# Hybrid GLA / neighbourhood / GQA backbone on one core: four split buffer pairs, low parts in halves, an estimated clock with the shared port, and regrouped GLA output products

## The chip, the cores and the metric

The kernel runs on one core of a Trainium2 chip. The metric is the time on the device, in microseconds, of one execution of the whole program. The profile is of one such execution, taken by the hardware profiler. Engines are named as the profile names them: PE is TensorE (its weight loads are PEld), DVE is VectorE, ACT is ScalarE, POOL is GpSimd, SP is SyncE, which issues most DMAs.

## The reference

Two layers of a diffusion backbone are computed over 256 latent tokens (x) and 256 context tokens (ctx) of width 1024. One layer is:

```
x = x + 0.5 * g1 * swiglu(modulate(rms_norm(x), sh1, sc1))          # FFN of width 2816; the same for ctx
p = modulate(rms_norm(x), sh2, sc2) @ w_in                          # 10784 columns
y = sum over 3 branches of sigmoid(gate_i) * (branch_i(p) @ w_branch[i]),  then @ w_out
x = x + g2 * y
x = x + 0.5 * g3 * swiglu(modulate(rms_norm(x), sh3, sc3))          # second FFN
```

The branches are a gated linear attention in both directions (GLA, 4 heads, chunks of 64 tokens), a neighbourhood attention (16 heads) and a grouped-query attention with rotary positions (GQA, 8 heads). The shifts, scales and gates come from `silu(c) @ w_mod + b_mod`, 9216 columns for each layer ("mods" below). In the second layer the context tokens are needed as keys and values alone. All is float32.

## The kernel before, in words

Tokens stand on the free axis, features on the partitions, so a weight tile of 128 x 128 is loaded into PE and 512 or 256 token columns are streamed. Float32 products of full precision are made from three products of the faster type float32r: each operand is split into a rounded high part and a low part (value minus high part), and `mm3` issues high x high, high x low and low x high into one PSUM bank.

Weights arrive in 504 chunks of 128 x 1024 (the `w_raw` tiles, 512 KB; a few are half as long). For each chunk `splitter` in `Program.run` lets ACT write the high part (`w_hi`, a cast) and POOL the low part (`w_lo`, one subtraction of 1024 columns a partition; in the first four chunks four of 256). `SPLIT_BUFS` = 3 pairs of `w_hi` and `w_lo` buffers go round, so the cast of a chunk waits until PE is done with the chunk three before it. `SPLIT_AHEAD` = 2 says how many chunks the recording may run ahead. Three raw buffers (`RAW_BUFS`) go round in front of that. Where a pair of chunks is needed at once (the first chunks of an FFN, the q and k projections of GLA in `proj_f2`, the last projection of `merge_out`), a chunk is marked "kept", and its buffers come free one chunk later.

The main line of the program is a list of chunks, each with the matmuls that use it (`up` and `dn` in the FFN, `pf` and `pt` in the projections). All else is a "side": generators for the mods (`mod_gen`, whose sums `mod_acc` are made on DVE), the norms (`norm_chain`), the splits of activations, the GLA heads (`gla_head`) and the attention heads (`attn_weights`, `attn_values`, with `head_norm` ahead of them). After every few matmuls `tick` asks every side whether its next instruction may be recorded now. That is decided by an estimated clock (class `Clock`): `took` gives each instruction a duration, `emit` adds it to its engine's time, and `Gated` lets a side's instruction in when its operands are ready by that clock (on PE with a margin of 0.5 us). So the durations in `took` set the order in which all engines' instructions stand. That order is then fixed, and on the chip each engine runs its own list in order and waits by semaphores.

The names that the steps below use: `rs_*` are the tiles of `rsqrt` (some ten small DVE operations, one behind the other), `a_s` the scores of attention in PSUM, `a_mx` their maxima, `a_p` the weights, `a_t` their transposes, `n_tab` the neighbourhood tables that POOL makes, `g_o` the outputs of GLA (`out_mm` in `gla_head`), `ff_h` the FFN's hidden values. Small tiles of 2 KB a partition come from one pool of `SLOTS` = 54.

Of the kernel before, what the change touches and what calls it, by code (L numbers as in the profile page):

```python
# [18 lines left out]
P = 128  # L19
# [17 lines left out]
C_GATE = 7712  # L37

RAW_BUFS = 3
SPLIT_BUFS = 3  # L40
SPLIT_AHEAD = 2
SLOTS = 54
LANES = 2
PE_MARGIN = 0.5
OTHER_SLACK = 0.1
QUEUE = 1.0
MOD_PACE = 42.0


def r32(ap):  # L50
    return ap.bitcast(F32R)


class Clock:
# [59 lines left out]
    def took(self, engine, name, ins, outs):  # L114
        n = max([x.free_size() for x in ins + outs] + [1])
        if engine == "PE":
            return 0.11 if name == "transpose" else self.matmul(ins, outs[0])
        if engine == "ACT":
            return 0.18 + n / 1200 + (0.2 if len(outs) > 1 else 0.0)
        if engine == "POOL":  # L120
            return 0.1 + n * 0.00235
        both = sum(not x.space == bass.MemoryType.PSUM and x.free_size() > 64 for x in ins) > 1
        return 0.15 + n / 960 * (1.8 if both else 1.15)

    def emit(self, engine, name, ins, outs):
        start = max(self.t[engine], self.need(ins, outs))
# [74 lines left out]
class Program:  # L201
# [155 lines left out]
    def run(self):  # L357
        specs = [it[1] for it in self.items if it[0] == "c"]
        raws, parts, ended = {}, {}, {}
        state = {"loaded": 0, "ci": 0}  # L360

        def load(n):
            while state["loaded"] < min(len(specs), n):
                j = state["loaded"]
                src, a, b = specs[j][:3]
                raw = self.rpool.tile([P, a, b], F32, name="w_raw", tag="r", padded_shape=[P, 1024 // b, b])
                old = raws.get(j - RAW_BUFS)
                if old is not None:
                    self.clock.floor[raw.name] = self.clock.read.get(old.name, 0.0)
                self.clock.dma(raw)  # L370
                self.nc.sync.dma_start(raw, src)
                raws[j] = raw
                state["loaded"] += 1

        def splitter():
            for j, (src, a, b, do, halves) in enumerate(specs):
                while j > state["ci"] + SPLIT_AHEAD or (j >= SPLIT_BUFS and j - SPLIT_BUFS not in ended):
                    yield None
                load(j + 1)
                hi = self.wpool.tile([P, a, b], F32, name="w_hi", tag="w", padded_shape=[P, 1024 // b, b])  # L380
                lo = self.wpool.tile([P, a, b], F32, name="w_lo", tag="w", padded_shape=[P, 1024 // b, b])
                self.clock.floor[hi.name] = self.clock.floor[lo.name] = ended.get(j - SPLIT_BUFS, 0.0)
                raw = raws[j]
                yield from self.gact.copy(r32(hi), raw)
                h = a // 4 if halves else a
                for s in range(0, a, h):
                    yield from self.ggp.tensor_tensor(r32(lo[:, s : s + h]), raw[:, s : s + h], hi[:, s : s + h], op=ALU.subtract)
                parts[j] = (r32(hi), r32(lo))
                load(j + 1 + RAW_BUFS)
                if self.force:  # L390
                    yield None

        self.load = load
        split = splitter()

        def advance(g):

            self.first = True
            self._resume(g)
            self.first = False  # L400

        work = self.round

        def round_with_splits():
            n = self.clock.count
            advance(split)
            w = list(self.wakes)
            more = work()
            self.wakes += w
            return more or self.clock.count > n  # L410

        self.round = round_with_splits
        for kind, _, fn in self.items:
            if kind == "f":
                self.flush()
                fn()
                continue
            ci = state["ci"]
            load(ci + 1)
            self.force = True  # L420
            while ci not in parts:
                advance(split)
            self.force = False
            fn(parts.pop(ci))
            if ci + 1 not in self.kept:
                ended[ci] = self.clock.now
            if ci in self.kept:
                ended[ci - 1] = self.clock.now
            state["ci"] = ci + 1
        self.flush()  # L430
        assert not self.sides, list(self.sides)
# [3 lines left out]
def tile_backbone(ctx: ExitStack, tc: tile.TileContext, I: dict, out: bass.AP):  # L435
# [4 lines left out]
    sml = ctx.enter_context(tc.tile_pool(name="sml", bufs=4))  # L440
    slot = ctx.enter_context(tc.tile_pool(name="slot", bufs=SLOTS))
    upool = ctx.enter_context(tc.tile_pool(name="upool", bufs=16))
    rpool = ctx.enter_context(tc.tile_pool(name="rpool", bufs=RAW_BUFS))
    wpool = ctx.enter_context(tc.tile_pool(name="wpool", bufs=2 * SPLIT_BUFS))
    psa = ctx.enter_context(tc.tile_pool(name="psa", bufs=4, space=PS))
# [10 lines left out]
    def S(name):  # L456
        return slot.tile([P, 512], F32, name=name, tag="s")
# [20 lines left out]
    def side_bank(name):  # L478
        t = psd.tile([P, 512], F32, name=name, tag="d")
        if getattr(prog, "floors", None):  # L480
            clock.floor[t.name] = max(prog.floors)
        return t
# [4 lines left out]
    def gmm(o, a, b, start, stop):  # L487
        yield from gpe.matmul(o, a, b, start=start, stop=stop)
# [58 lines left out]
    x = [cst.tile([P, NT], F32, name=f"x{k}") for k in range(KT)]  # L547
# [201 lines left out]
    def mod_side(blocks):  # L749
        st["mod_done"] = set()  # L750
        prog.start(
            "mods", lambda: (mod_gen(blocks[i : i + 2], "mods", MOD_PACE) for i in range(0, len(blocks), 2))
        )
# [486 lines left out]
    def gla_head(l, h, nq):  # L1240
# [4 lines left out]
        v = [st["gv"][t, h // 2][:, (h % 2) * 256 : (h % 2) * 256 + 256] for t in range(TT)]  # L1245
# [131 lines left out]
        at = S("g_at")[:, :nq]  # L1377
        yield from gdve.tensor_tensor(at, att[0], att[1], op=ALU.add)

        state = [dict(), dict()]  # L1380
# [23 lines left out]
        ss = sml.tile([P, TT], F32, name="g_ss", tag="g_ss")  # L1404

        def out_mm(t):
            if t % 2 == 0:
                on[t // 2] = side_bank("g_o")
            po = on[t // 2][:, (t % 2) * 256 : (t % 2) * 256 + 256]
            yield from gmm(po, at[:, t * P : (t + 1) * P], v[t], True, False)  # L1410
            todo = [(half, d) for d in range(2) for half in range(2) if t in state[d]]
            for i, (half, d) in enumerate(todo):
                lhs = qe[d][:, (2 * t + half) * 64 : (2 * t + half + 1) * 64] if half == d else qe2[d][:, t, :]
                yield from gmm(po[64 * half : 64 * half + 64, :], lhs, state[d][t], False, i >= len(todo) - 2)

        def out_ev(tp):
            o = S("g_o32")
# [18 lines left out]
        for tp in reversed(range(ntq // 2)):  # L1436
            yield from prog.banks(1)
            for t in range(2):
                yield from out_mm(2 * tp + t)
            yield from out_ev(tp)  # L1440
            prog.release(1)
            yield from out_ss(tp)
# [588 lines left out]
    for l in range(DEPTH):  # L2031
        last = l == DEPTH - 1
        n = LAT if last else NT
# [51 lines left out]
```

## Time and profile before

| | |
|---|---|
| median of 3 runs | 2831.05 us (2829.24 to 2831.47) |
| the profiled execution's own time | 2831.27 us |
| its span in the profile | 2829.5 us |
| PE busy | 2767.3 us, 98% |
| PE weight loads busy | 2316.6 us, 82% |
| DVE busy | 1669.3 us, 59% |
| ACT busy | 1011.8 us, 36% |
| POOL busy | 1279.1 us, 45% |
| HBM read | 342.83 MB, mean 122 GB/s |
| mean granted TensorE clock | 0.994 of full speed |

The span runs from the first to the last instruction. Busy time is the time in which an engine has an instruction under way, also when that instruction itself is held up. What PE does not spend busy is time in which it waited for something; the profile names what ended each wait. The granted clock is given for each stretch as a share of 2.4 GHz, so a stretch at 1.2 GHz reads 0.50.

### The profile page before, as it was taken

Reading aid. Unit: us, or ns where it says so; the run is one execution under the profiler, and the core shown is the slowest. Engines: PE = TensorE matmul, PEld = TensorE weight load, DVE = VectorE, ACT = ScalarE, POOL = GpSimd, SP = SyncE. Lnnn points to the kernel's source line nnn. Section 1 sums busy time; section 2 is a strip of 40 time slices with the busy share of each in tenths; the row PEclk is TensorE's granted clock in tenths of the full one; section 3 lists DMA queues with packets and bytes.
Section 4 is the critical chain, followed back from the end, with each engine's and each line's share of the span. In section 5 each row is a group of like instructions: output and inputs, shape, how many; then the busy total and the mean of one; then the engine's idle time right before and its main releaser. Section 6 shows DMA issues by size and latency. Waiting matters only on the chain.

```text
span 2829.5 us, 39683 instructions
## 1 busy us (share of the span) xinstructions
PE 2767.3 (98%) x15547; PEld 2316.6 (82%) x15547; DVE 1669.3 (59%) x2956; ACT 1011.8 (36%) x1603; POOL 1279.1 (45%) x591
## 2 busy tenths in 40 slices
PE   8999999999999999999999999999999998999999
PEld 6888888777777788888888888888877777899899
DVE  5655566678766675667555475512554659756422
ACT  3222223433544344322222222222244335564443
POOL 4444442334333443334444434444333455557687
PEclk9999999999999999999999999999999999999999
DMA  7444443224222322433444434433322334435554
GB/s 247 150 145 140 149 138 98 90 82 133 74 74 66 88 75 60 154 129 124 137 142 144 157 116 141 135 97 116 89 78 80 103 102 118 119 105 193 169 183 157
DMA packets 295839, 346.46 MB, mean 122 GB/s; under 512 B 15669, under 2 KB 239062, under 8 KB 295652
## 3 DMA queue, kind: packets, MB, share of 16 engines
q1 hardware_dynamic: 295252, 343.81, 38.8%
q8 instruction: 122, 2.00, 0.3%
q14 instruction: 65, 0.53, 0.1%
q10 hardware_dynamic: 176, 0.07, 0.0%
q0 software_dynamic: 224, 0.05, 0.0%
HBM read 342.83 MB, written 1.05 MB: 122 GB/s over the span
## 4 chain that ended last, share of the span: by engine, by line
PE 87%; DVE 9%; issue 3%; POOL 1%; DMA 1%; ACT 0%; SPq 0%; DVEq 0%; ACTq 0%; POOLq 0%
PE up L169 29%; PE pf L169 17%; PE dn L169 15%; PE pt L169 14%; PE a_s L196 2%; PE a_t L196 2%; PE n_o L196 1%; PE g_o L196 1%; PE q_o L196 1%; POOL w_lo L196 1%; PE g_U L196 1%; DVE a_p L196 1%; DVE n_ss L196 1%; PE a_qk L196 1%; DVE rs_y L196 1%
## 5 line engine op out<-in xcount | busy, mean ns | idle before, releaser
L196 POOL TENSOR_TENSOR w_lo<-w_raw,w_hi 128x1024 fp32r<-128x1024 f32 (+2 forms) x516 | 1219.5, 2369 | 1487.1 <-ACT w_hi L196 1431.5
L196 ACT CAST w_hi<-w_raw 128x1024 fp32r<-128x1024 f32 (+1 forms) x504 | 520.8, 1036 | 945.2 <-issue 286.9
L169 PE MATMUL up<-u_hi,w_hi 128*128 128x512 f32 (+1 forms) x1504 | 530.9, 353 | 2.2 <-DVE u_hi L196 2.1
L169 PE MATMUL up<-u_hi,w_lo 128*128 128x512 f32 (+1 forms) x1504 | 528.7, 352 | 4.0 <-POOL w_lo L196 3.9
L169 PE MATMUL up<-u_lo,w_hi 128*128 128x512 f32 (+1 forms) x1504 | 529.8, 352 | 2.8 <-DVE u_lo L196 2.2
L196 DVE SCALAR_TENSOR_TENSOR mod_acc<-mod_w,scv,mod_acc 128x512 f32<-128x512 f32 x364 | 374.8, 1078 | 53.2 <-DMA mod_w<-w_mod 53.2
L169 PE MATMUL dn<-ff_h,w_hi 128*128 128x512 f32 (+1 forms) x1528 | 397.0, 349 | 0.0
L169 PEld LDWEIGHTS up<-u_hi,w_hi 128*128 128x128 f32 x1504 | 285.2, 190 | 50.4 <-issue 6.7
L169 PEld LDWEIGHTS up<-u_hi,w_lo 128*128 128x128 f32 x1504 | 285.1, 190 | 42.5 <-POOL w_lo L196 5.2
L169 PEld LDWEIGHTS up<-u_lo,w_hi 128*128 128x128 f32 x1504 | 285.2, 190 | 42.2 <-DVE u_lo L196 4.7
L169 PEld LDWEIGHTS dn<-ff_h,w_hi 128*128 128x128 f32 x1528 | 267.5, 189 | 39.8 <-issue 2.5
L169 PE MATMUL dn<-ff_h,w_lo 128*128 128x512 f32 (+1 forms) x764 | 265.9, 348 | 0.0
L169 PE MATMUL pt<-w_hi,u_hi 128*128 128x512 f32 x640 | 261.8, 409 | 0.0
L169 PE MATMUL pf<-u_hi,w_hi 128*128 128x256 f32 (+1 forms) x736 | 250.8, 341 | 5.7 <-DVE u_hi L196 2.2
L169 PE MATMUL pt<-w_hi,u_lo 128*128 128x512 f32 x640 | 251.2, 393 | 0.0
L169 PE MATMUL pt<-w_lo,u_hi 128*128 128x512 f32 x640 | 251.0, 392 | 0.0
L169 PE MATMUL pf<-u_lo,w_hi 128*128 128x256 f32 (+1 forms) x736 | 239.5, 325 | 3.7 <-DVE u_lo L196 2.9
L169 PE MATMUL pf<-u_hi,w_lo 128*128 128x256 f32 (+1 forms) x736 | 238.2, 324 | 4.2 <-POOL w_lo L196 4.2
L169 DVE TENSOR_TENSOR ff_h<-ff_a,up 128x512 f32<-128x512 f32 (+1 forms) x88 | 53.3, 621 | 311.6 <-PE up L169 278.9
L169 PE MATMUL pf<-y,w_hi 128*128 128x512 f32 (+1 forms) x768 | 197.4, 347 | 2.0 <-ACT y L196 1.2
L169 PEld LDWEIGHTS pf<-u_hi,w_hi 128*128 128x128 f32 x736 | 141.8, 193 | 27.3 <-issue 8.3
L169 PEld LDWEIGHTS dn<-ff_h,w_lo 128*128 128x128 f32 x764 | 144.6, 189 | 18.2
(229 smaller groups left out, 3937.9 us busy)
## 6 DMA issues: line engine op xcount, KB each, us to landing
w_raw<-ffn_w_in SPq DMA_DIRECT2D x176, 512.0 KB
w_raw<-w_in SPq DMA_DIRECT2D x168, 512.0 KB
mod_w<-w_mod SPq DMA_DIRECT2D x288, 256.0 KB
w_raw<-ffn_w_out SPq DMA_DIRECT2D x80, 512.0 KB
w_raw<-w_branch SPq DMA_DIRECT2D x48, 512.0 KB
w_raw<-w_out SPq DMA_DIRECT2D x16, 512.0 KB
w_raw<-ffn_w_out SPq DMA_DIRECT2D x16, 256.0 KB
n_rel<-nat_rpb SPq DMA_DIRECT2D x32, 109.5 KB
```

The lines of the kernel that those rows point to most:

```text
L169: return real(*args, **kw)
L196: return real(*args, **kw)
```

## The change

- `SPLIT_BUFS` goes from 3 to 4 and `SPLIT_AHEAD` from 2 to 3: four pairs of split buffers. To make room, `SLOTS` goes from 54 to 52.
- The low part of every chunk is made in two subtractions of half the columns (the first four chunks keep their four).
- The estimated clock gives a DVE instruction 0.15 us plus its elements at 960 per us times 1.1, and another 0.15 us (`PORT_WAIT`) where `shares` finds that all its tensors lie in SBUF and that it reads two of them, or that it is a `tensor_scalar` or a `tensor_copy`. Before, it was 0.15 us plus the elements times 1.8 for two wide SBUF inputs and times 1.15 otherwise.
- In `out_mm` of GLA the product of an odd token tile with 128 output partitions (`at` with `v`) is issued last, behind its products with 64 output partitions, where it was issued first. The start and stop flags move with it.

```diff
-SPLIT_BUFS = 3
-SPLIT_AHEAD = 2
-SLOTS = 54
+SPLIT_BUFS = 4
+SPLIT_AHEAD = 3
+SLOTS = 52
...
+PORT_WAIT = 0.15
...
-        both = sum(not x.space == bass.MemoryType.PSUM and x.free_size() > 64 for x in ins) > 1
-        return 0.15 + n / 960 * (1.8 if both else 1.15)
+        return 0.15 + n / 960 * 1.1 + (PORT_WAIT if self.shares(name, ins, outs) else 0.0)
+
+    @staticmethod
+    def shares(name, ins, outs):
+
+        tensors = [x for x in ins if x.free_size() > 1]
+        if any(x.space == bass.MemoryType.PSUM for x in tensors + outs):
+            return False
+        return len(tensors) > 1 or bool(tensors) and name in ("tensor_scalar", "tensor_copy")
...
-                h = a // 4 if halves else a
+                h = a // 4 if halves else a // 2
...
             po = on[t // 2][:, (t % 2) * 256 : (t % 2) * 256 + 256]
-            yield from gmm(po, at[:, t * P : (t + 1) * P], v[t], True, False)
+            if t % 2 == 0:
+                yield from gmm(po, at[:, t * P : (t + 1) * P], v[t], True, False)
             todo = [(half, d) for d in range(2) for half in range(2) if t in state[d]]
             for i, (half, d) in enumerate(todo):
                 lhs = qe[d][:, (2 * t + half) * 64 : (2 * t + half + 1) * 64] if half == d else qe2[d][:, t, :]
-                yield from gmm(po[64 * half : 64 * half + 64, :], lhs, state[d][t], False, i >= len(todo) - 2)
+                first, last = i < 2 and t % 2 == 1, i >= len(todo) - 2 and t % 2 == 0
+                yield from gmm(po[64 * half : 64 * half + 64, :], lhs, state[d][t], first, last)
+            if t % 2 == 1:
+                yield from gmm(po, at[:, t * P : (t + 1) * P], v[t], False, True)
```

The new durations move instructions all through the program. Three places show how.

PE, one pair of GLA output tiles in the first layer, before:

```order
L196 MATMUL g_o<-g_v,g_at 128x256
L196 MATMUL g_o<-g_S,g_qe 64x256
L196 MATMUL g_o<-g_S,g_half 64x256 x2
L196 MATMUL g_o<-g_S,g_qe 64x256
L196 MATMUL g_o<-g_v,g_at 128x256
L196 MATMUL g_o<-g_S,g_qe 64x256
L196 MATMUL g_o<-g_S,g_half 64x256 x2
L196 MATMUL g_o<-g_S,g_qe 64x256
```

and now:

```order
L204 MATMUL g_o<-g_v,g_at 128x256
L204 MATMUL g_o<-g_S,g_qe 64x256
L204 MATMUL g_o<-g_S,g_half 64x256 x2
L204 MATMUL g_o<-g_S,g_qe 64x256 x2
L204 MATMUL g_o<-g_S,g_half 64x256 x2
L204 MATMUL g_o<-g_S,g_qe 64x256
L204 MATMUL g_o<-g_v,g_at 128x256
```

The eight products with 64 output partitions now stand together, between the two with 128. There are 12 such pairs in the program, and in the changed one nothing stands between their products.

ACT, the second layer, where the GLA gates' projection `fg` has come out and the q and k projections of the next heads begin, before:

```order
654 L169 CAST fg<-fg 32x512 x2
655 L196 CAST w_hi<-w_raw 128x1024
656 L196 ACTIVATE g_abs<-g_z 128x512 x3
657 L196 ACTIVATE g_abs<-g_abs 128x512 x3
658 L196 ACTIVATE g_abs<-g_z 128x512
659 L196 ACTIVATE g_abs<-g_abs 128x512 x4
660 L196 ACTIVATE g_e<-g_G 128x512
661 L196 ACTIVATE g_ei<-g_G 128x512
662 L196 ACTIVATE g_abs<-g_abs 128x512
663 L196 CAST w_hi<-w_raw 128x1024 x2
664 L196 ACTIVATE g_e<-g_G 128x512
```

and now:

```order
660 L177 CAST fg<-fg 32x512 x2
661 L204 CAST w_hi<-w_raw 128x1024
662 L204 ACTIVATE g_abs<-g_z 128x512 x3
663 L204 ACTIVATE g_abs<-g_abs 128x512 x3
664 L204 ACTIVATE g_abs<-g_z 128x512
665 L204 ACTIVATE g_abs<-g_abs 128x512 x4
666 L204 ACTIVATE g_e<-g_G 128x512
667 L204 ACTIVATE g_ei<-g_G 128x512
668 L204 ACTIVATE g_abs<-g_abs 128x512
669 L204 CAST w_hi<-w_raw 128x1024
670 L204 ACTIVATE g_e<-g_G 128x512
```

The rows read alike, but the casts are of later chunks now: counted over ACT's whole list, 332 chunks are cast ahead of the `g_abs` rows where it was 331; at the same place in the first layer it is 80 where it was 79.

DVE, the second layer, behind the rotary `rsqrt` chain of the GQA keys, where two neighbourhood heads have their maxima made (ISA is the fused addition of the table and maximum), before:

```order
1856 L196 TENSOR_TENSOR q_raw<-q_raw,rs_y 128x256 x4
1857 L196 TENSOR_TENSOR q_sw<-q_raw,cossin 128x128 x2
1858 L196 TENSOR_TENSOR q_rot<-q_raw,cossin 128x256
1859 L196 TENSOR_REDUCE a_mx<-a_s 128x1
1860 L196 ISA a_s,a_mx<-a_s,n_tab,a_mx 128x256
1861 L196 ISA a_mx 128x1
1862 L196 TENSOR_SCALAR a_mx<-a_mx 128x1
1863 L196 TENSOR_REDUCE a_mx<-a_s 128x1
1864 L196 TENSOR_TENSOR q_rot<-q_rot,q_sw 128x256
```

and now:

```order
1846 L204 TENSOR_TENSOR q_raw<-q_raw,rs_y 128x256 x4
1847 L204 TENSOR_TENSOR q_sw<-q_raw,cossin 128x128 x2
1848 L204 TENSOR_TENSOR q_rot<-q_raw,cossin 128x256
1849 L177 COPY q_raw<-pt 128x512
1850 L204 TENSOR_REDUCE a_mx<-a_s 128x1 x2
1851 L204 TENSOR_TENSOR q_rot<-q_rot,q_sw 128x256
1852 L204 ISA a_s,a_mx<-a_s,n_tab,a_mx 128x256
1853 L204 ISA a_mx 128x1
1854 L204 ISA a_s,a_mx<-a_s,n_tab,a_mx 128x256
1855 L204 ISA a_mx 128x1
```

The two heads' first scores stand together on PE now, and so do their maxima here. On PE, counted over its list, the two groups of scores of those maxima had 6 `pt` products between them and 30 behind the second until the next scores; now they stand next to each other with 48 behind them.

## Rows read from the trace of the kernel before

**Rows 1.** Page, part 1: busy us (share of the span) xinstructions.

```profile
PE 2767.3 (98%) x15547; PEld 2316.6 (82%) x15547; DVE 1669.3 (59%) x2956; ACT 1011.8 (36%) x1603; POOL 1279.1 (45%) x591
```

**Rows 2.** Windows, PE alone: stretch, length, busy us (x), granted clock, DMA share, GB/s.

```profile
0.00:42.00 42.00, 33.86 (x209) 1.00 0.95 328
406.00:426.00 20.00, 17.50 (x129) 1.00 0.42 119
...
2026.00:2045.00 19.00, 15.20 (x89) 0.91 0.31 87
462.00:490.00 28.00, 24.66 (x191) 0.94 0.30 94
1655.00:1668.00 13.00, 11.42 (x81) 0.87 0.32 103
2074.00:2098.00 24.00, 20.09 (x149) 0.93 0.22 66
2636.00:2642.00 6.00, 4.29 (x35) 1.00 0.23 68
436.00:450.00 14.00, 12.57 (x62) 1.00 0.56 160
...
2300.00:2620.00 320.00, 301.20 (x2211) 0.97 0.45 134
2328.00:2345.00 17.00, 11.45 (x40) 0.80 0.38 113
```

**Rows 3.** Waits of PE, longest first: us in total, times, longest us.

```profile
PE a_s L196 <- ACT a_p L196: 8.1, 3, 3.2
...
PE pf L169 <- POOL w_lo L196: 4.2, 3, 2.0
...
PE pf L169 <- DVE fg L169: 1.8, 2, 0.9
```

**Rows 4.** Timeline, PE, one GLA output pair of layer two: start us, us, instruction.

```profile
2111.49 0.59 PE L196 MATMUL g_o<-g_v,g_at 128*128 128x256 f32 x2
2112.02 0.43 PE L196 MATMUL g_o<-g_S,g_qe 128*64 128x256 f32 x1
...
2112.51 0.38 PE L196 MATMUL g_o<-g_S,g_qe 128*64 128x256 f32 x1
...
2112.72 0.38 PE L196 MATMUL g_o<-g_S,g_qe 128*64 128x256 f32 x1
2113.03 0.70 PE L196 MATMUL g_o<-g_v,g_at 128*128 128x256 f32 x2
2113.66 0.43 PE L196 MATMUL g_o<-g_S,g_qe 128*64 128x256 f32 x1
```

**Rows 5.** Timeline, ACT and PE, 2074 to 2098 us; in brackets idle before, and releaser.

```profile
2088.19 1.99 ACT L196 CAST w_hi<-w_raw 128x1024 fp32r<-128x1024 f32 x2
...
2091.78 0.39 PE L169 MATMUL pf<-u_hi,w_lo 128*128 128x256 f32 x1 [1.99 <-POOL w_lo L196]
```

**Rows 6.** Timeline, DVE and POOL, 2322 to 2329 us.

```profile
2323.65 0.17 DVE L196 TENSOR_TENSOR rs_a<-rs_y,rs_a 128x8 f32<-128x8 f32 x1
2323.85 2.38 DVE L196 SCALAR_TENSOR_TENSOR rs_y<-rs_a,rs_y 128x8 f32<-128x8 f32 x1
2326.26 2.32 DVE L196 TENSOR_TENSOR rs_a<-rs_y,rs_v 128x8 f32<-128x8 f32 x1
...
2323.80 4.75 POOL L196 TENSOR_TENSOR w_lo<-w_raw,w_hi 128x1024 fp32r<-128x1024 f32 x2 [0.62 <-ACT w_hi L196]
```

**Rows 7.** Instructions by tile, DVE: ns min/median/max, first and last start, forms.

```profile
L196 DVE TENSOR_TENSOR ff_h<-ff_h,ff_h x88: 409/1371/2897, 55.9 to 2796.8; 128x512 fp32r<-128x512 f32 x66, 128x256 fp32r<-128x256 f32 x22
```

**Rows 8.** Groups by shape, POOL, whole span: xcount, busy us, mean ns, idle before.

```profile
L196 POOL TENSOR_TENSOR w_lo<-w_raw,w_hi 128x1024 fp32r<-128x1024 f32 x484 | 1185.2, 2453 | 1441.3 <-ACT w_hi L196 1395.6 <-PE g_oT L196 15.6 <-PE q_o L196 8.0
```

**Rows 9.** The same view, 2647 to 2829 us, the last FFN.

```profile
L196 POOL TENSOR_TENSOR w_lo<-w_raw,w_hi 128x1024 fp32r<-128x1024 f32 x59 | 142.4, 2416 | 31.1 <-ACT w_hi L196 26.7 <-DMA w_raw<-ffn_w_out 1.8 <-PE dn L169 1.4
L196 POOL TENSOR_TENSOR w_lo<-w_raw,w_hi 128x512 fp32r<-128x512 f32 x4 | 5.2, 1290 | 0.0
```

## The prediction

> **What bounds the kernel now.** I read the page's busy times first: PE is busy for 2767.3 of 2829.5 us, so the end is set by PE's list, and apart from cheaper PE work only its idle time, 62.2 us, can be won [rows 1]. The reader should then see where that idle time lies. A table of windows with PE alone gives idle (length less busy) and granted clock for each [rows 2].
>
> - Start, 0 to 42 us: 8.1 us, on first loads.
> - Four stretches behind norms (first 406 to 426, last 2026 to 2045): 2.5, 3.2, 1.3 and 3.8, together 10.7 us.
> - Four stretches behind "kept" pairs (462, 1655, 2074, 2636): 3.3, 1.6, 3.9 and 1.7, together 10.5 us.
> - Four stretches of GLA and attention (436 to 450, 490 to 1150, 2098 to 2300, 2300 to 2620): 1.4, 5.1, 2.1 and 18.8, together 27.4 us. Nearly a third of the last lies in one place: 5.55 idle in 2328 to 2345.
>
> A long wait costs twice. In 2328 to 2345 the granted clock is 0.80 on average, that is part of it at 1.2 GHz, after PE had stood still. What the clock took from a stretch is its length times one less the clock: 28 x 0.06 + 13 x 0.13 + 24 x 0.07 = 5.0 us behind kept pairs, 320 x 0.03 = 9.6 us in the last attention stretch, 19 x 0.09 = 1.7 us behind the last norm [rows 2]. The waits view names releasers: ACT `a_p` for the scores, 8.1 us, POOL `w_lo` for projections, 4.2 us, and DVE `fg` twice, 1.8 us [rows 3].
>
> **The change, part by part.**
>
> *GLA products.* In the timeline of one pair, a product with 64 output partitions starts 0.21 after the one before (2112.51 to 2112.72), but the step out of such products to a 128 one takes 0.31 (to 2113.03), and the two 128 products behind it take 0.63 (to 2113.66) where the first two took 0.53 (2111.49 to 2112.02) [rows 4]. So crossing costs 0.10 on leaving and 0.10 on arrival, and I take 0.09 for going back, as the nearest. The regrouping removes one round trip in each of the 12 pairs: 12 x 0.29 = **3.5 us**, all on PE. The order shows the 64 products standing together, so I see no bound worse than 3.0.
>
> *Four pairs.* In the stretch at 2074 to 2098, ACT's casts start at 2088.19 only, behind the whole `g_abs` block of the order's rows, and PE waits 1.99 us for the `w_lo` that follows [rows 5]. With four pairs, one more chunk is cast ahead of that block, as the counts with the order show. A chunk lasts PE about 24 x 0.12 = 2.9 us at 256 columns (35 products in 4.29 us [rows 2]), more than the waits there. Of the 10.5 us idle behind kept pairs, 1.8 are the two waits for `fg` [rows 3], which stay. The rest with its clock is 8.7 + 5.0 = 13.7 us. The bounds are 0, if the cast is late for another reason too, and 13.7; I take **11**, nearer to the upper, because the order moves exactly this cast. On SP's queue, loads of chunks move ahead of loads of the mods, by one chunk as a rule, and two slots fewer of 54 may let a load of the mods or a write wait longer for its slot. Both delay what is now off PE's path. I take nothing, the lower bound, and for the upper one the 8.1 us that the start loses to loads now [rows 2].
>
> *Halved low parts.* This is the main part. In 2323 to 2329, DVE operations on 8 elements take 2.38 and 2.32 us, while the one just before took 0.17, and their ends (2326.23, 2328.58) are where the first and second of two POOL instructions of 2.4 us end [rows 6]. A DVE instruction with two inputs in SBUF stands still until the POOL instruction under way is done. `ff_h` shows it too: 409 at least, 1371 in the median, 2897 at most [rows 7]. With halves of about 1.29 us (the 512 column form in the last FFN [rows 9]) the longest such wait falls from 2.4 to 1.3, and the mean with it. Of the 27.4 us idle in GLA and attention, plus 9.6 of clock, 37.0 in all, I let half go: **18.5**. Bounds: 0 and 37.
>
> The price: a chunk takes 2 x 1.290 = 2.58 instead of 2.42 to 2.45 [rows 8, 9], 0.13 to 0.16 each, some 60 to 80 us of POOL over 484 chunks. It is covered: POOL is busy 45% [rows 1], and its idle time there is 1441.3 us, mostly for ACT [rows 8]. The thinnest cover is the last FFN, where it waits 31.1 us in 182 [rows 9]. There the halves take 59 x 0.16 = 10 us of that. Were that cover gone, each chunk over 2.9 us would hold PE up.
>
> One rule speaks against this part. The rows show that DVE got in between two POOL instructions that stood back to back: the second long one begins at 2326.26, after the first POOL instruction's end [rows 6]. The Trainium skill (GPSIMD Engine Reference, section 2.1, Instruction dispatch) says that POOL's cores begin their part of the next instruction as soon as they are through with their part of this one, without waiting for each other. If the port therefore never came free between two halves, halving would shorten no wait; the trace has it otherwise for whole chunks. By the rule the sum would be the first rival's.
>
> *The estimated clock.* A two-input operation of 512 elements now counts 0.15 + 0.59 + 0.15 = 0.89 us, before 1.11; a `tensor_scalar` 0.89, before 0.76; each small operation of a `rsqrt` chain 0.15 more. At the place of the 5.55 us stall, the chain counts longer, so PE gets 48 `pt` products behind the scores where it had 30. That cover helps the stall along with the halves, and is in the 18.5. But the whole order is a new draw, and new waits will arise where none was. Nothing in the trace prices them; the bounds are 0 and as much as is there now (27.4). I take **7**, a quarter.
>
> **The sum.** -3.5 - 11 - 18.5 + 7 = -26. Against the profiled execution's own 2831.27 us, which lies 0.2 above the median of 2831.05, that is **2805 us**. The start, the norms (their operations have an operand in PSUM and run at one length) and the end stay.
>
> **The rivals.**
>
> *The halves shorten no wait.* POOL keeps the port over both halves, or DVE is just held twice. For it: back to back halves come right after each other. Against it: [rows 6]. Then only products and pairs gain: 2831.3 - 14.5 = 2817 us.
>
> *Slower: the new durations are too short for two-input operations.* `ff_h` would take, with half the waiting, about 0.68 + 0.47 = 1.15 us in its 512 form, where the clock now counts 0.89 and counted 1.11. PE's sides are then let in too early in all stretches of GLA and attention, and its list stands still more often, each time with the lower clock behind it. Half as many stalls again as now would be +18.5, so 2831.3 - 14.5 + 18.5 = 2835 us. It decides from 14.5 us of new stalls, that is 39% over the 37.0. For it: every gap of PE in [rows 3] for `a_p` stems from a count that was too short. Against it: for `tensor_scalar` and the small chains the new counts are longer, and these stand before the largest stalls.
>
> *POOL becomes the bound in the last FFN.* DVE instructions that are under way first would hold up two POOL starts in each chunk. At 1.60 us a half, 59 x (3.20 - 2.90) = 18 us comes back there: 2805 + 18 = 2823 us. It decides from 1.45 us a half; the form now takes 1.29 [rows 9]. The Trainium skill (SBUF — State Buffer, section Who interferes with whom) has it that whoever starts first keeps the shared port for its whole instruction; the DVE row of 2.38 us agrees for one side [rows 6], and no row read here shows the other.
>
> **How the numbers follow.** Forecast 0.70, no shorter waits 0.13, durations too short 0.12, POOL the bound 0.05. A measurement of this kernel can tell about 0.2% from no change, 5.7 us. The forecast's own range is 2787 to 2824: down to all of the pairs' 13.7 and 27 of the 37, with no new waits (2831.3 - 3.5 - 13.7 - 27 = 2787), up to pairs and products and little else. The range of 8 in 10 takes in the first and third rivals and the better part of the second: 2787 to 2831. Faster by over 0.2%: 0.70 less a little at its upper end, and most of the first and third rivals, 0.79. Within 0.2%: 0.08. Slower: 0.13.
>
> **What would show it.** Right: POOL busy some 1340 to 1370 us with the 512 form near 1.3; the longest DVE waits near 1.3 to 2.0 and DVE busy under 1560; PE waits for `w_lo` near nothing; `g_o` pairs near 2.9 us where one takes 3.2; PE busy lower by 3 and by clock, its idle near 45. Wrong: DVE operations of 8 elements that still take 2.3 us; as many PE waits for `a_p`, `a_t` as before; POOL without idle time in the last FFN; or PE waits of over 2 us at new places.

## The result and the profile after

The changed kernel takes **2815.2 us** in the median of 6 runs (2813.0 to 2816.5), the kernel before 2830.8 in runs beside it (2829.0 to 2831.5). The ratio is 0.9946, with a 95% interval of 0.9936 to 0.9957: 15 us, or 0.5%, faster. The forecast was 2805, in a range of 2787 to 2831. One execution each of runs 5 and 10 below took over 8000 us, and their medians leave it out.

The page of the changed kernel, part 1, answers to [rows 1] (its line 204 is line 196 of before, and 177 is 169):

```profile
PE 2759.8 (98%) x15547; PEld 2314.2 (82%) x15547; DVE 1613.4 (57%) x2948; ACT 1014.5 (36%) x1611; POOL 1422.4 (51%) x1091
```

The span is 2812.3 us, so PE idles for 52.5 us where it idled for 62.2. Of the 17 us that the span lost, 9.7 are idle time and 7.5 cheaper PE work, part of it clock. POOL is busy 143 us longer; forecast were 60 to 80.

The windows of PE answer to [rows 2]: the two stretches behind kept pairs in the projections, and attention.

```profile
460.00:490.00 30.00, 29.09 (x222) 1.00 0.30 95
```

```profile
2070.00:2095.00 25.00, 24.10 (x196) 1.00 0.22 65
...
2300.00:2610.00 310.00, 294.00 (x2194) 0.97 0.46 140
```

Behind the kept pairs only one wait of 0.9 us is left at each place, and the clock stays at 1.00 there. Attention still idles for 16.0 us (18.8 before), at the same clock. The waits answer to [rows 3]:

```profile
PE a_s L204 <- ACT a_p L204: 9.7, 5, 5.1
PE a_t L204 <- DVE a_p L204: 5.4, 4, 3.8
```

No wait of `pf` for `w_lo` stands in the list any more, but the two waits for `a_p` are as long as before, 15.1 us together where they were 8.1 and 5.8. On DVE and POOL, by tile and by shape, against [rows 7] and [rows 8]:

```profile
L204 DVE TENSOR_TENSOR ff_h<-ff_h,ff_h x88: 495/1370/1779, 57.9 to 2780.0; 128x512 fp32r<-128x512 f32 x66, 128x256 fp32r<-128x256 f32 x22
```

```profile
L204 POOL TENSOR_TENSOR w_lo<-w_raw,w_hi 128x512 fp32r<-128x512 f32 x968 | 1324.9, 1392 | 1285.1 <-ACT w_hi L204 1261.9 <-PE a_s L204 12.7 <-PE mod L204 5.2
```

The longest `ff_h` fell from 2.90 to 1.78 us, the median stayed. A half takes 1.39 us in the mean, so a chunk takes 2.78 where it took 2.45. The longest wait of PE, 5.1 us, stands behind this piece of the timeline of DVE and POOL, the start and the end of the `rsqrt` chain and the product behind it, here and then before:

```profile
2303.93 0.49 DVE L204 TENSOR_SCALAR rs_v<-h_ss 128x8 f32<-128x8 f32 x1
...
2316.94 1.21 DVE L204 SCALAR_TENSOR_TENSOR rs_y<-rs_a,rs_y 128x8 f32<-128x8 f32 x1
2318.18 5.75 DVE L204 TENSOR_TENSOR q_raw<-q_raw,rs_y 128x256 f32<-128x256 f32 x4
```

```profile
2306.30 5.03 POOL L204 TENSOR_TENSOR w_lo<-w_raw,w_hi 128x512 fp32r<-128x512 f32 x4
...
2313.09 10.57 POOL L204 TENSOR_TENSOR w_lo<-w_raw,w_hi 128x512 fp32r<-128x512 f32 x8
```

```profile
2314.53 1.51 DVE L196 TENSOR_SCALAR rs_v<-h_ss 128x8 f32<-128x8 f32 x1
...
2328.82 0.17 DVE L196 SCALAR_TENSOR_TENSOR rs_y<-rs_a,rs_y 128x8 f32<-128x8 f32 x1
2329.02 1.43 DVE L196 TENSOR_TENSOR q_raw<-q_raw,rs_y 128x256 f32<-128x256 f32 x4
```

POOL runs halves back to back, eight in its last row. Operations of the `rsqrt` chain are held, that is, they stand still until the POOL instruction under way is done: nine of the 13 take 1.2 to 1.3 us, about one half, where four took 2.3 to 2.4 us before [rows 6]. From its first `rs_v` to the end of the last `rs_y` the chain takes 14.2 us; before it took 14.5. The product behind it takes 5.75 us, before 1.43.

That made the first theory after the result: **halving makes holds shorter and more frequent, and is worth nothing**; the gain would be pairs and products. The first four runs tested it.

### The profile page after: what moved, and what is told of

It reads as the page before. It is cut to its first block, busy times and chain, and to the rows that moved or that the text cites. A ratio compares the mean times of both kernels' runs of the same rounds, so it can differ in the third digit from the quotient of the medians.

```text
span 2812.3 us, 40615 instructions
## 1 busy us (share of the span) xinstructions
PE 2759.8 (98%) x15547; PEld 2314.2 (82%) x15547; DVE 1613.4 (57%) x2948; ACT 1014.5 (36%) x1611; POOL 1422.4 (51%) x1091
## 4 chain that ended last, share of the span: by engine, by line
PE 75%; DVE 6%; ACT 1%; issue 0%; DMA 0%; POOL 0%; DVEq 0%; SPq 0%; ACTq 0%; POOLq 0%
PE up L177 21%; PE pf L177 19%; PE pt L177 13%; PE dn L177 11%; PE a_s L204 2%; PE a_t L204 2%; PE n_o L204 1%; PE g_o L204 1%; PE q_o L204 1%; PE g_U L204 1%; PE a_qk L204 1%; DVE n_ss L204 1%; DVE u_hi L204 1%; DVE u_lo L204 1%; DVE rs_a L204 0%
## 5 line engine op out<-in xcount | busy, mean ns | idle before, releaser
L204 POOL TENSOR_TENSOR w_lo<-w_raw,w_hi 128x512 fp32r<-128x512 f32 (+1 forms) x1016 | 1363.7, 1365 | 1332.6 <-ACT w_hi L204 1309.4
L204 DVE SCALAR_TENSOR_TENSOR mod_acc<-mod_w,scv,mod_acc 128x512 f32<-128x512 f32 x364 | 348.6, 1005 | 67.7 <-DMA mod_w<-w_mod 67.6
L177 PEld LDWEIGHTS up<-u_hi,w_hi 128*128 128x128 f32 x1504 | 284.3, 189 | 52.5 <-issue 5.9
```

Source lines behind the costliest of these rows:

```text
L177: return real(*args, **kw)
L204: return real(*args, **kw)
```

## Experiments

Intervals are at 95%, ratios against runs of the kernel before on the same chip; "us" behind a ratio is that ratio against 2830.8. In the runs with halves added or taken away alone, the recording counts each low part as before, so that PE, DVE, ACT and SP keep the order of the kernel that is named.

**1. Halves alone**, in the order of before.

```diff
-h = a // 4 if halves else a
+h = a // 4 if halves else max(1, a // 2)
...
+clock.emit("POOL", "tensor_tensor", [raw, hi], [r32(lo)])
+for s in range(0, a, h):
+    self.nc.gpsimd.tensor_tensor(...)
```

> The kernel before, with the low part of every chunk made in two halves; the lists of PE, DVE, ACT and SP stand exactly as in the kernel before, and only POOL's list has twice the subtractions. Theory (a hold is halved in length, but a chain of DVE operations is now held in every half, so holds double in number): no change that can be told, 2826 to 2836 us, against 2830.8 before; POOL's w_lo takes 100 to 150 us more in total (2.7 to 2.8 us a chunk); PE's waits for a_p and a_t together stay within 3 us of before. Rival (the prediction's term: half of the 37 us goes): 2812 us, 2805 to 2820, and PE's waits for a_p and a_t fall by half.

Measured: 2806.4 us, ratio 0.9914 (0.9900 to 0.9928), **-24 us**. The theory fell. The waits of PE, two of before and then this run's:

```profile
PE a_t L196 <- DVE a_p L196: 5.8, 5, 2.7
...
PE a_t L196 <- DVE a_pt L196: 2.6, 1, 2.6
```

```profile
PE a_s L196 <- ACT a_p L196: 8.2, 4, 3.1
...
PE pf L169 <- POOL w_lo L368: 1.8, 2, 0.9
...
PE a_t L196 <- DVE a_p L196: 0.6, 1, 0.6
```

Waits for `a_t` went from 5.8 us (and 2.6 for `a_pt`) to 0.6; those of `pf` for `w_lo` from 4.2 to 1.8, since the first products need the first half alone. Waits of `a_s` stayed at 8.2; the chain ahead of them takes 14.3 us here, in the order of before, and took 14.5. One place shows how the gain comes about. DVE in the kernel before, and then the same instructions here:

```profile
2356.42 2.93 DVE L196 TENSOR_TENSOR gg_w<-gg_w,g_oT 128x256 f32<-128x256 f32 x2
...
2361.55 2.91 DVE L196 TENSOR_TENSOR y<-gg_w,y 128x256 fp32r<-128x256 f32 x2
```

```profile
2350.01 0.75 DVE L196 TENSOR_TENSOR gg_w<-gg_w,g_oT 128x256 f32<-128x256 f32 x2
...
2351.90 1.84 DVE L196 TENSOR_TENSOR y<-gg_w,y 128x256 fp32r<-128x256 f32 x2
```

Behind the second row PE waited 2.64 us for `a_pt` before; here that wait is gone. The clock pays as well: the span is 23.0 us shorter, of which 13.9 are PE's idle time (62.2 to 48.3) and 9.1 its busy time, at the same instructions and a mean granted clock of 0.997 after 0.994.

**2. The changed kernel with whole low parts**, in its own order.

```diff
-h = a // 4 if halves else a // 2
+h = a // 4 if halves else a
...
-return 0.1 + n * 0.00235
+return (0.2 if n == 1024 else 0.1) + n * 0.00235
```

The second line lets the estimated clock count a whole low part as long as two halves, so that the order stays.

> The changed kernel with whole low parts again; the lists of PE, DVE, ACT and SP stand exactly as in the changed kernel. Theory (halves are worth nothing): 2811 to 2820 us, against 2815.2 for the changed kernel; POOL busy back to some 1280 us. Rival (the prediction's term): 2833 us, 2827 to 2841. A second rival (the new order's counts fit halves alone: a tensor_scalar at 0.89 us is too short where a hold lasts 2.4): over 2822 us, with new waits of PE for DVE in the attention stretches.

Measured: 2833.6 us, ratio 1.0010 (1.0002 to 1.0019). So halves are worth 18 us in the changed order, and without them the change is no gain at all. In the waits, `a_p` shows:

```profile
PE a_s L204 <- ACT a_p L204: 12.5, 5, 5.3
PE a_t L204 <- DVE a_p L204: 8.8, 5, 4.8
```

**3. Four pairs alone** (`SPLIT_BUFS` 4, `SPLIT_AHEAD` 3, `SLOTS` 52 in the kernel before).

> The kernel before with four split buffer pairs, three chunks ahead and 52 slots, and nothing else. Theory (all that stands behind kept pairs goes, waits and clock): 2817 us (2814 to 2821), and no wait of PE for w_lo outside the start. Rival (the pairs gain the 8.7 us of idle only, or the deeper queue of POOL work holds DVE elsewhere and gives some back): 2822 to 2831 us.

Measured: 2831.5 us, ratio 1.0000 (0.9991 to 1.0009). The theory fell, and with it the forecast's 11 us. The waits of `pf` for `w_lo` behind kept pairs did go; a new one came, and in all PE idles 65.1 us, before 62.2. The waits of PE, then DVE, POOL and PE around it:

```profile
PE a_s L196 <- ACT a_p L196: 8.8, 3, 3.9
PE g_oT L196 <- DVE g_o L196: 7.9, 3, 4.6
```

```profile
2137.99 2.28 DVE L196 TENSOR_TENSOR rs_a<-rs_y,rs_v 128x2 f32<-128x2 f32 x1
...
2140.50 2.24 DVE L196 SCALAR_TENSOR_TENSOR rs_y<-rs_a,rs_y 128x2 f32<-128x2 f32 x1
...
2142.96 2.27 DVE L196 TENSOR_TENSOR rs_a<-rs_y,rs_a 128x2 f32<-128x2 f32 x1
```

```profile
2137.84 4.87 POOL L196 TENSOR_TENSOR w_lo<-w_raw,w_hi 128x1024 fp32r<-128x1024 f32 x2 [1.95 <-ACT w_hi L196]
2142.88 2.34 POOL L196 TENSOR_TENSOR w_lo<-w_raw,w_hi 128x1024 fp32r<-128x1024 f32 x1 [0.16 <-ACT w_hi L196]
```

```profile
2146.55 0.45 PE L196 MATMUL g_oT<-ident,g_o 128*128 128x128 f32 x1 [4.65 <-DVE g_o L196]
```

Three low parts fall into GLA's output norm. In the kernel before, POOL was idle there:

```profile
2138.57 2.40 POOL L196 TENSOR_TENSOR w_lo<-w_raw,w_hi 128x1024 fp32r<-128x1024 f32 x1 [9.74 <-PE g_oT L196]
```

Its 9.74 us of idle time had covered the chain (2133.29 to 2135.70) by chance: ACT's cast, which POOL needs, stood in ACT's list behind its work on `g_oT`, `g_o` and `g_v` and began at 2137.44 only. A wait that cost nothing on POOL had kept DVE from being held.

**4. GLA products alone.**

> The kernel before with the GLA products regrouped and nothing else. Theory (12 round trips of 0.29 us less on PE): 2827.3 us (2826 to 2829), PE busy 3 us lower. Rival (the changed order around the products makes another wait, or the step back costs nothing): 2829.5 to 2833 us.

Measured: 2825.9 us, ratio 0.9982 (0.9973 to 0.9991), **-5 us**. A part of one pair of the changed kernel, PE, against [rows 4]:

```profile
2112.29 0.38 PE L204 MATMUL g_o<-g_S,g_qe 128*64 128x256 f32 x1
2112.59 0.70 PE L204 MATMUL g_o<-g_v,g_at 128*128 128x256 f32 x2
2113.13 0.49 PE L204 MATMUL g_kt<-ident,g_kx 128*128 128x128 f32 x3
```

Behind the last 128 product the next work of 128 follows at once. From the first product of each group to the instruction behind it, all pairs take 30.6 us in this run and 35.0 before: 4.4 us, or 0.37 a pair (0.43 in the four pairs with the fewest products), where I had 0.29. The products of a pair do not all stand together, as I had said of the change: in the four pairs of the changed kernel's second layer, of which this is one, six `pt` products stand behind the first products, and the rest follow at 2111.15.

**5. Halves and products, without pairs and durations.**

> The kernel before with halved low parts and the regrouped GLA products, without the four pairs and without the new durations; order as in the kernel before, apart from the rows around the products. Theory (halves and products add up: 24 to 25 us and 5 us): 2801 us, 2798 to 2805, faster than the changed kernel's 2815. Rival (the products' 5 us were partly waits for DVE, which the halves shorten anyway): 2804 to 2807 us.

Measured: **2801.4 us**, ratio 0.9892 (0.9877 to 0.9908), in the theory's range. This is the fastest version, 14 us below the changed kernel by the medians. Its attention stretch and its waits:

```profile
2300.00:2600.00 300.00, 291.75 (x2203) 0.99 0.49 148
```

```profile
PE a_s L196 <- ACT a_p L196: 5.8, 3, 3.1
```

That is 8.3 us idle at clock 0.99, where the changed kernel idles 16.0 at 0.97.

**6. The new durations alone.**

> The kernel before with the new durations of DVE in the estimated clock and nothing else. Theory (the new order by itself loses): 2838 us, 2833 to 2843, with PE waits for a_p and a_t together over 18 us where they are 14 before. It follows from the changed kernel with whole low parts, 2833.6, plus the products' 5 us, with nothing for the pairs. Rival (the durations are neutral, and it is pairs and durations together that lose): 2828 to 2833 us.

Measured: 2835.3 us, ratio 1.0013 (1.0004 to 1.0022), +4 us. The time is the theory's, the waits are not:

```profile
PE a_s L204 <- ACT a_p L204: 8.2, 4, 4.1
PE a_t L204 <- DVE a_p L204: 7.1, 5, 4.7
```

That is 15.3 us in total where the theory had over 18, and PE's idle time in all is 61.3 us, not more than before; 4.4 us more stand in its busy time (2771.7), and why stays open. The longest wait for `a_t`, 4.75 us from 2563 on, is longer than any for it before (2.7); the changed kernel has it too, here its PE and ACT and then DVE:

```profile
2547.03 1.54 PE L204 MATMUL a_s<-a,a 128*128 128x512 f32 x6
2552.35 0.48 PE L204 MATMUL a_t<-ident,a_p 128*128 128x128 f32 x1 [3.78 <-DVE a_p L204]
```

```profile
2550.80 0.69 ACT L204 ACTIVATE a_p<-a_s,a_mx 128x512 f32<-128x512 f32 x1 [2.50 <-DVE a_mx L204]
```

```profile
2548.50 1.42 DVE L177 TENSOR_TENSOR z<-z,m_w 128x256 f32<-128x256 f32 x1
2549.84 0.68 DVE L204 TENSOR_REDUCE a_mx<-a_s 128x1 f32<-128x512 f32 x1
```

The maxima stand behind two `z` additions, and PE's list holds nothing between the scores and the transposes. The first addition took 0.42 us, the second, held, 1.42.

**7. Pairs and halves**, in the order of run 3.

> The kernel before with four pairs (as in the run with pairs alone, same order) and halved low parts. Theory (halves already take the waits behind the kept pairs, so pairs have nothing left to win, and their order makes waits of PE for g_o of GLA): 2806 to 2814 us, not below the 2806.4 of halves alone. Rival (the halves also shorten the waits that the pairs made elsewhere, and the pairs' 13.7 us come through in part): 2793 to 2803 us.

Measured: 2812.1 us, ratio 0.9929 (0.9916 to 0.9942), in the theory's range: 4 us above halves alone, which the two intervals (some 5 us together) don't tell from nothing. At the place of run 3, DVE, POOL and PE:

```profile
2134.04 1.16 DVE L196 TENSOR_TENSOR rs_a<-rs_y,rs_v 128x2 f32<-128x2 f32 x1
...
2136.49 1.21 DVE L196 SCALAR_TENSOR_TENSOR rs_y<-rs_a,rs_y 128x2 f32<-128x2 f32 x1
```

```profile
2133.89 7.52 POOL L368 TENSOR_TENSOR w_lo<-w_raw,w_hi 128x512 fp32r<-128x512 f32 x6 [1.80 <-ACT w_hi L196]
```

```profile
2142.54 0.30 PE L196 MATMUL g_oT<-ident,g_o 128*128 128x128 f32 x1 [4.59 <-DVE g_o L196]
```

Six holds of 1.2 us in place of three of 2.3, and the wait is 4.59 us after 4.65. So the first theory holds in one case, a dependent chain inside a burst of POOL work. In sum halving still wins: this run is 20 us below run 3.

**8. The changed kernel with three pairs** (3, 2 and 54 again).

> The changed kernel with three pairs, two chunks ahead and 54 slots as before, so halves, products and new durations alone. Theory (pairs are worth nothing beside halves, the durations carry the loss): 2811 to 2820 us. Rival (the pairs carry the loss): 2798 to 2807 us. A second rival (the pairs are worth their 8.7 to 13.7 us in the changed kernel): 2824 to 2829 us.

Measured: 2816.9 us, ratio 0.9944 (0.9931 to 0.9957): as the changed kernel. Beside halves, products and durations, pairs are worth nothing that can be told.

Against run 5 this run has more than the new durations, since its recording counts every low part as two instructions, as the changed kernel's does. Its order is neither run 5's nor run 6's. At the long chain, run 6 has the two groups of scores six `pt` products apart, and here and in the changed kernel they stand together. PE's wait there, run 6 and then this run:

```profile
2336.78 0.50 PE L204 MATMUL a_s<-a,a 64*128 64x512 f32 x1 [2.11 <-ACT a_p L204]
```

```profile
2329.49 0.79 PE L204 MATMUL a_s<-a,a 64*128 64x512 f32 x1 [5.08 <-ACT a_p L204]
```

**9. Quarters** instead of halves in run 5 (`h = max(1, a // 4)`; chunks of two row blocks stay in halves, among them those around 2320 us, so the two waits named are no test).

> As the run with halves and products (2801.8 us; no four pairs, no new durations, same order of PE, DVE, ACT and SP), but the low part of each chunk in quarters. Theory (halving helped where PE waited behind one held DVE operation, and those waits are gone; a chain of small operations in a burst of POOL work is caught once in every piece, and gains nothing by shorter pieces): 2799 to 2807 us, the two waits of PE for a_p near 2320 us still 4.5 to 6 us together, POOL 150 to 250 us busier. Rival (waits go on falling with the length of a hold): 2788 to 2796 us, those two waits under 3.5 us. A second rival (a chunk now costs POOL over the 2.9 us that PE has for it in the FFNs): over 2812 us.

Measured: 2811.2 us, ratio 0.9927 (0.9915 to 0.9940), 10 us above run 5 and in nobody's range but near the second rival's. DVE's `ff_h` by tile, and one instance of it and POOL in the last FFN:

```profile
L196 DVE TENSOR_TENSOR ff_h<-ff_h,ff_h x88: 412/822/14852, 56.5 to 2773.5; 128x512 fp32r<-128x512 f32 x66, 128x256 fp32r<-128x256 f32 x22
```

```profile
2725.78 15.14 DVE L196 TENSOR_TENSOR ff_h<-ff_h,ff_h 128x256 fp32r<-128x256 f32 x2 [2.65 <-ACT ff_h L196]
```

```profile
2714.49 25.82 POOL L368 TENSOR_TENSOR w_lo<-w_raw,w_hi 128x256 fp32r<-128x256 f32 x37
```

One subtraction was held for 14.8 us, until POOL's burst of quarters, whose last 37 the row shows, ended at 2740.31; 20 of them had started behind it. A second one was held as long at 2667. PE waited 1.51 us for `ff_h` at the first place, so these holds are not the whole difference.

**10. A fourth pair of buffers under run 5's order**, with 52 slots.

> The run with halves and products, with a fourth pair of buffers alone: the recording still counts three pairs, so every engine's list stands as in that run, and 52 slots. Theory (the pairs' loss came from the order, in which casts stand ahead of the GLA activations and POOL then runs in the norm chains): 2796 to 2802 us, with no new wait of PE for g_o. Rival (the loss comes from the buffers themselves: casts start earlier and POOL falls into the chains): 2804 to 2809 us.

Measured: 2806.8 us, ratio 0.9913 (0.9897 to 0.9928), in the rival's range and 5 to 6 us above run 5, which is as much as the two intervals leave to chance. Waits for `q_rot` and `g_o`, both made by DVE, grew from 1.6 and 0.6 us to 2.2 and 1.9:

```profile
PE a_qk L196 <- DVE q_rot L196: 2.2, 1, 2.2
PE g_oT L196 <- DVE g_o L196: 1.9, 3, 1.2
```

These 1.9 us are not the whole difference. Whether the rest is the buffers or the two slots fewer stays open.

**11 and 12. PE's margin** at 1.0 and at 0.75 in run 5, where it is 0.5.

> The run with halves and products, with PE's margin in the estimated clock at 1.0 us where it is 0.5, so that PE's sides are let in half a microsecond later and have that much more cover. Theory (PE's waits for a_p, g_la, g_o come from counts that were too short, more margin covers them): 2794 to 2800 us. Rival (a new order is a new draw and makes as many waits as it covers): 2801 to 2810 us.

> The same with PE's margin at 0.75 us. Theory (more margin covers waits): 2796 to 2802 us, between the runs with 0.5 and with 1.0. Rival (a new draw): anywhere from 2797 to 2812 us, in no order with the other two.

Measured: 2818.1 (ratio 0.9951, 0.9939 to 0.9964) and 2806.5 us (0.9910, 0.9897 to 0.9924). Both are above run 5, 17 and 5 us; the 5 are within the intervals, the first is above everybody's range and the second in the rival's. More margin in the estimate covered no more: with 1.0, waits for `g_o` are back (4.2 us, in run 5 0.6), and the mean granted clock is 0.995 where it is 0.997 in run 5. The theory fell.

## Why the prediction was right or wrong

The total lay in the range and on the right side, but it came from terms that were off in both directions, so that it was right is in part luck. By the total alone, 2815, the rival by which halves shorten no wait (2817) was nearer than the forecast (2805); only runs 1 and 2, with halves added and taken away, decide against it. The runs stack up from before to the changed kernel, each step read from its ratio:

| step | forecast, us | measured, us |
|---|---|---|
| halves (run 1) | -18.5 | -24 |
| products (run 5 over run 1) | -3.5 | -6 (-5 alone) |
| new durations, new order (run 8 over run 5) | +7 | +15 (+4 alone, run 6) |
| four pairs (after over run 8) | -11 | +1 (0 alone, +4 beside halves) |
| sum | -26 | -15 |

Each measured step is uncertain by some 4 to 6 us.

- **The pairs' 11 us are the step that failed.** Its mechanism was right for its place: the waits behind kept pairs, and the low clock behind them, went. But I took pairs as adding to the halves, while halves take much of the same waits (run 1, `w_lo` 4.2 to 1.8 us), and I took the lower bound as 0. I costed what is late next only for loads on SP's queue, not for POOL's low parts themselves: a cast one chunk earlier starts a low part one chunk earlier, and that holds DVE. Run 3 shows the bill, 7.9 us of PE waits for `g_o` where there was 1.0.
- **The new order's 7 us were a quarter of a bound, and too small.** Next to halves it costs 15, the count of two instructions a chunk included; alone, in another order, it costs 4 (run 6), and how the 15 divide stays open. The largest stalls of the new order are of the kind that halving shortens least: the chain at 2303 to 2324 (5.31 and 1.29 us of PE waits whole, 5.13 and 1.30 in halves) and the transposes with nothing ahead of them (4.75 whole, 3.78 in halves). That fits the 24 us that halves are worth in the old order and the 18 in the new. I had counted the 48 products behind the scores as cover for the first; in the changed kernel it is PE's longest wait.
- **Halves: the mechanism was right, the size too small**, 24 for 18.5, partly because they also shorten what I had given to the pairs. The sign that I named for it, DVE waits of 1.3 to 2.0 us at most, came (`ff_h` 1.78); DVE busy under 1560 did not (1613), since holds became more frequent. That sign was the wrong one: DVE's total says little, PE's waits behind single operations say it. PE's idle time, 52.5 us, missed the 45 too, and one sign of being wrong did come, waits for `a_p` as long as before: the new order's stalls hide there what the halves took away, which run 1 shows.
- **POOL's price** was 143 us instead of 60 to 80: I priced a half as it runs in the last FFN before (1.29), and it runs at 1.39 in the mean. It was covered, as forecast: in the last FFN PE is busy 168.35 of 172 us (2640 to 2812), so that rival fell.
- **The rule against the halves** (the Trainium skill, GPSIMD Engine Reference, section 2.1: cores begin their part of the next instruction without waiting for each other) does not keep DVE out between halves: in run 7 six operations of the chain, 1.16 to 1.24 us each, pass beside six halves. With quarters the long hold that I feared came (14.8 us, run 9); whether that rule is its cause stays open.
- **The slower rival** said that the new counts let PE's sides in too early. Runs 6 and 8 agree with its sign, and run 8's 15 us come near its 18.5. It fell because it had the halves gain nothing, and they gained 24.

## What to carry to other kernels

Before giving an engine more room to run ahead, look for the engine that its instructions hold up, and for the places where its own waits now leave that engine free; the room is paid there. Cutting a long instruction that holds another engine helped the operations that met it one by one, not a dependent chain inside a burst, and with quarters the pieces at times let the other engine in no more. Terms that shorten the same wait don't add up, and in a program whose order comes from estimates each edit must be timed alone and beside the others: here two of four edits made the result slower or no faster.

## What the runs showed of the hardware

- Twice in run 9 a burst of POOL subtractions of 256 columns kept a DVE subtraction of two SBUF tensors standing for 14.8 us, over 20 pieces each time. Beside pieces of 512 columns the same operation never took over 1.8 us (changed kernel, runs 1 and 5), and in run 7 DVE got in six times of six. The burst's row gives 25.82 / 37 = 0.70 us from one piece to the next, and the median piece lasts 0.74, so pieces overlap. For halves it is 7.52 / 6 = 1.25 against 1.29, also an overlap; what makes the difference between the two stays open.
- DVE holds POOL too: a half takes 1.29 us in the median, 1.39 in the mean of the changed kernel. In run 1 the longest, 2.79 us from 584.11 on, began while five DVE operations with two SBUF inputs each ran one behind the other from 583.51 to 585.75.
